# The mixers' sample products on whole zero-padded operands, level products regrouped, diagonal scores from a ones product

## The chip, the core and the metric

The kernel runs on one NeuronCore of a Trainium2 chip. That core has five engines with a queue each: TensorE (PE; its weight loads are shown as PEld), VectorE (DVE), ScalarE (ACT), GpSimd (POOL) and SyncE (SP), which here only issues DMAs. The metric is the device time of one execution in microseconds (us), lower is better.

## The reference, cut to what matters

One inference step of a two-layer encoder. Two sequences go through the same weights: a prompt of 256 frames and a sample of 32 frames, which continues a stream with a recurrent state and cached keys and values. Each layer is a half SwiGLU, a mixer, and another half SwiGLU, each on normalised input and added to x. Layer 0 has the mixer AB: 8 HGRN2 heads and 8 stick-breaking attention heads side by side. Layer 1 has the mixer C, a gMLP with a spatial product over positions.

```
# HGRN2, blocks of positions; c = cumulative sum of log f, k = 1 - f
scores = einsum('bthc,btshc,bshc->bhts', q, decay, k)       # s <= t
o      = scores @ v + (q * exp(c)) @ S
S_new  = exp(c_last) * S + (k * exp(c_last - c))^T @ v
# stick-breaking: A[t,s] = sigmoid(z_ts) * prod_{s<j<t} (1 - sigmoid(z_tj)), o = A @ v
# gMLP: mixed = ws @ layernorm(v) + b ; out = (u * mixed) @ w_out
```

All is float32 to the outside. The outputs are y of both sequences, the new keys and values, the new HGRN states and the sample's normalised v rows.

## The kernel before, in words

Activations lie with features on the 128 partitions and the NT = 288 tokens in the columns: columns 0 to 31 are the sample, 32 to 287 the prompt's two blocks of 128. Weights are streamed from DRAM in chunks of up to 8 x 128 rows and 256 columns; ScalarE and VectorE split every chunk into a rounded part `wh` and a rest `wl` (lines 169 and 170), and for each 128x128 block TensorE makes three products with 288 columns (lines 209 to 211: `wl` with the rounded activations, `wh` with their rest, `wh` with the rounded ones) into `acc`. These are 9216 products, and they are called weight products below.

The mixers' own work runs beside them in lanes: generators (`hgrn`, `stick_keys`, `stick`, `spatial`) of which a step is taken every so many row blocks of a chunk (`tick`, line 187). A step issues a few small products, which so stand as a short block between two weight products in TensorE's queue, and the work of the other engines around them. The order of every queue is fixed when the program is built (a scheduler may move instructions that don't depend on each other); at run time each engine takes its queue in order and waits on semaphores.

In mixer AB there are four head pairs p. For each, `hgrn` makes:

- the diagonal of the scores (lines 537 to 540): per head b, a product of k and q for each of the prompt's two blocks and one of 32x32 for the sample, of which only the diagonal is kept (lines 543, 544). The second prompt block has its sources back to front, for which `kr` holds k mirrored;
- seven levels m = 1 to 64 (`scores`, line 511): per head one product of 128x128x128 for the prompt and, in the five levels up to m = 16, one with a stationary of 32 columns for the sample (line 518), in turn head by head; `place` puts them into `sc` and `ss` by a mask;
- the states (line 579) from decayed keys `kt` and values `vt`, the outputs (lines 594 to 598), and their transposes back (line 617). The sample's share of these takes 32 rows (or columns) of a tile only: `ROWS = (P, P, TS)`.

`stick_keys` transposes the normalised keys (line 672, again 128, 128 and 32 rows), `stick` sums the sample's queries' squares (line 706, after head 1's transposes and squares) and `weighted` makes the outputs, where the sample's new values are a stationary of 32 rows (line 776). In mixer C, `spatial` multiplies the normalised v with the spatial weights: two products of 128x128x128 for the prompt (line 895) and one with 32 rows for the sample (line 896), in 16 blocks.

A product of two float32 operands that are not rounded is recorded as two matmuls, a transpose and a weight product as one. The matmul's shape in a row is written rows*columns of the stationary operand in the array.

Of the kernel before, what the change touches and what calls it, by code (L numbers as in the profile page):

```python
# [10 lines left out]
AF = mybir.ActivationFunctionType  # L11
# [15 lines left out]
LEVELS = (1, 2, 4, 8, 16, 32, 64)   # HGRN: block lengths; up to 16 a mask picks the blocks  # L27
NM = 5

# token windows of 128 columns: the prompt's blocks, and one that the sample leads  # L30
WIN = ((32, 160), (160, 288), (0, 128))
ROWS = (P, P, TS)


def shape_constants():
    """Masks and identity: they depend on shapes alone."""
    ident = np.eye(P, dtype=np.float32)
    s = np.arange(P)[:, None]
    t = np.arange(P)[None, :]
    ge = (s <= t).astype(np.float32)          # [query, key]: key >= query  # L40
# [6 lines left out]
    # level masks [source, target of a second half]; the second block's sources are back to front  # L47
# [11 lines left out]
class Lane:  # L59
    """Work that runs beside the weight products, a step at a time."""  # L60
# [19 lines left out]
class Net:  # L80
# [66 lines left out]
    def fetch_half(self, j):  # L147
        """The first chunk, half of its rows at a time."""
# [6 lines left out]
    def pieces(self, i):  # L155
        """The steps that split chunk i, a few row blocks each."""
# [30 lines left out]
    def tick(self):  # L187
        """Between row blocks: the next chunk's split and the lanes' steps go on."""
# [7 lines left out]
    def mm(self, acc, ch, rhs, order, first, last, blocks=(0, 1)):  # L196
        """acc[:, b] (+)= the chunk's column block b times rhs; order: (row block, rhs block)."""
# [36 lines left out]
    def put(self, k, h):  # L234
        """Two hidden blocks from k on, split into two parts."""
# [6 lines left out]
    def gained(self, k, x, g):  # L242
        """Block k of the next products' operand, gain * x, in two parts."""
# [5 lines left out]
    def square(self, k):  # L249
        """The squares' sum over the blocks of x; after the last, 1 / rms."""  # L250
# [11 lines left out]
    def rnorm(self, sq):  # L262
        """1 / rms of each token, on every partition: rb [128, 2, NT]."""
# [26 lines left out]
    def resid(self, j, b, acc, scale, gnext):  # L290
        """Block 2j + b of x takes the product up."""
# [17 lines left out]
    def out_proj(self, plan, scale, gnext, j0=0):  # L309
        """x += scale * (hidden @ w): plan: the K chunks' orders."""  # L310
# [41 lines left out]
    # column groups of ab_w_in, as they are taken: f, q, v, gate of HGRN; v, k, q of stick-breaking  # L352
# [14 lines left out]
    def mixer_ab(self, gnext):  # L367
        nc, I = self.nc, self.I
        with self.tc.tile_pool(name="ab", bufs=1, reuse_waits="tile") as pool:
# [10 lines left out]
            nc.gpsimd.memset(self.sk, 1.0)  # L380
            self.gk = T("gk", [P, P])
# [56 lines left out]
    def hgrn(self, p, pool, d):  # L438
        """Two heads. The prompt in two chunks of 128 positions, the sample in one of 32. In a chunk,
        decays between positions are products of f within blocks of m positions, m doubling:  # L440
        Pp[t] = f from t's block start through t, E[s] = f from after s to its block's end."""
# [24 lines left out]
        vt = T("vt", [P, 2, 384])  # L466
# [673 lines left out]
```

## Time and profile before

| what | value |
|---|---|
| time of one execution, 3 runs | 1382.73, 1382.88, 1384.78 us (median 1382.88) |
| span of the profiled execution, first to last instruction | 1381.3 us |
| TensorE, matmuls | 1374.0 us busy, 99% of the span, 10234 records |
| VectorE | 872.5 us, 63% |
| ScalarE | 658.8 us, 48% |
| GpSimd | 83.6 us, 6% |
| granted TensorE clock, mean | 1.000 |
| HBM traffic | 154 GB/s over the span |

The page has no execution time of the profiled run beside its span; the median of the timed runs is 1.6 us above the span. Busy time of an engine counts the union of its records. Matmuls overlap in the pipeline and their ends are modelled, so how long a product holds the queue is read from the starts of neighbouring records, not from a record's length.

### The profile page before, as it was taken

The page shows a single profiled execution, that of the slowest core. Times are in us where ns is not written, and L with a number is a line of the kernel's source. Part 1 is how long each engine was busy: PE and PEld are TensorE (multiplying, and loading weights), DVE is VectorE, ACT ScalarE, POOL GpSimd, SP SyncE. Part 2 cuts the span into 40 slices and gives each one's busy share as a digit, 9 for nine tenths or more (in the row PEclk, how much of TensorE's full clock was granted, in tenths as well). Part 3 has the DMA queues.
Part 4 walks back from the last instruction along what each step waited for, and adds up shares of the span by engine and source line. Part 5 has one row for each costly group of instructions (what it writes and reads, how often), then busy time and mean ns, then how long its engine had stood idle before and what let it go on. Part 6 is the DMA issues. An engine that isn't in the chain of part 4 may idle for free.

```text
span 1381.3 us, 24967 instructions
## 1 busy us (share of the span) xinstructions
PE 1374.0 (99%) x10234; PEld 1341.9 (97%) x10234; DVE 872.5 (63%) x1623; ACT 658.8 (48%) x1343; POOL 83.6 (6%) x133
## 2 busy tenths in 40 slices
PE   9999999999999999999999999999999999999998
PEld 8999999989898989999999999999999999999998
DVE  7666557767676756666665666655568865666643
ACT  6444445373736455544444444444554445444432
POOL 0000000010101010000000100000110910000000
PEclk9999999999999999999999999999999999999999
DMA  8454555343434334654545745454544445555451
GB/s 286 156 182 154 164 163 186 119 158 100 144 114 130 94 115 134 196 168 154 182 139 167 218 153 183 153 162 160 175 139 137 149 141 157 172 160 174 155 178 48
DMA packets 212788, 214.71 MB, mean 155 GB/s; under 512 B 4737, under 2 KB 211314, under 8 KB 212674
## 3 DMA queue, kind: packets, MB, share of 16 engines
q1 hardware_dynamic: 211314, 210.56, 47.7%
q0 software_dynamic: 672, 1.90, 0.5%
q8 instruction: 80, 1.31, 0.4%
q10 hardware_dynamic: 688, 0.66, 0.2%
q14 instruction: 34, 0.28, 0.1%
HBM read 208.25 MB, written 4.85 MB: 154 GB/s over the span
## 4 chain that ended last, share of the span: by engine, by line
PE 97%; ACT 1%; DMA 1%; DVE 1%; SPq 0%; issue 0%; POOL 0%; ACTq 0%
PE acc L209 30%; PE acc L211 29%; PE acc L210 29%; PE sc L515 1%; DMA wraw<-in_ffn_w_up_dram 1%; PE vt L126 1%; PE sp L895 1%; PE S L579 0%; PE sc L518 0%; ACT on L702 0%; PE sp L896 0%; PE kt L126 0%; ACT on L600 0%; PE zs L720 0%; PE oT L617 0%; PE kn L672 0%
## 5 line engine op out<-in xcount | busy, mean ns | idle before, releaser
L169 ACT CAST wh<-wraw 128x512 fp32r<-128x512 f32 x768 | 442.2, 619 | 540.8 <-PE acc L211 412.4
L170 DVE TENSOR_TENSOR wl<-wraw,wh 128x512 fp32r<-128x512 f32 x768 | 507.8, 688 | 270.1 <-ACT wh L169 269.8
L209 PE MATMUL acc<-xh,wl 128*128 128x288 f32 x2112 | 638.6, 302 | 0.0
L211 PE MATMUL acc<-xh,wh 128*128 128x288 f32 x2112 | 623.9, 295 | 0.0
L210 PE MATMUL acc<-xl,wh 128*128 128x288 f32 x2112 | 621.9, 294 | 0.0
L209 PEld LDWEIGHTS acc<-xh,wl 128*128 128x128 f32 x2112 | 397.4, 188 | 4.4 <-issue 1.4
L210 PEld LDWEIGHTS acc<-xl,wh 128*128 128x128 f32 x2112 | 398.4, 189 | 1.2 <-issue 0.5
L211 PEld LDWEIGHTS acc<-xh,wh 128*128 128x128 f32 x2112 | 397.3, 188 | 0.0
L209 PE MATMUL acc<-hh,wl 128*128 128x288 f32 x960 | 285.5, 298 | 0.0
L210 PE MATMUL acc<-hl,wh 128*128 128x288 f32 x960 | 283.1, 295 | 0.0
L211 PE MATMUL acc<-hh,wh 128*128 128x288 f32 x960 | 283.0, 295 | 0.0
L209 PEld LDWEIGHTS acc<-hh,wl 128*128 128x128 f32 x960 | 180.3, 188 | 1.1 <-issue 0.2
L210 PEld LDWEIGHTS acc<-hl,wh 128*128 128x128 f32 x960 | 180.5, 188 | 0.1
L211 PEld LDWEIGHTS acc<-hh,wh 128*128 128x128 f32 x960 | 180.3, 188 | 0.0
L227 DVE TENSOR_TENSOR u<-acc,rb 128x576 f32<-128x576 f32 x52 | 39.3, 756 | 52.1 <-PE acc L211 52.0
L227 DVE TENSOR_TENSOR g<-acc,rb 128x576 f32<-128x576 f32 x48 | 36.3, 757 | 49.1 <-PE acc L211 48.7
L238 ACT CAST hh<-u 128x576 fp32r<-128x576 f32 x52 | 35.1, 674 | 54.1 <-DVE u L347 39.3
L239 DVE TENSOR_TENSOR hl<-u,hh 128x576 fp32r<-128x576 f32 x52 | 39.6, 762 | 7.8 <-ACT hh L238 1.8
L119 POOL TENSOR_TENSOR pw<-ms,mhalf 128x3 f32<-128x3 f32 x6 | 6.4, 1069 | 534.5 <-DVE ms L272 515.9
L245 ACT ACTIVATE xh<-xT,cols 128x288 fp32r<-128x288 f32 x40 | 21.3, 532 | 26.7 <-DVE xT L298 15.4
L347 DVE TENSOR_TENSOR u<-u,g 128x576 f32<-128x576 f32 x44 | 33.1, 752 | 0.0
L345 ACT ACTIVATE g<-g 128x576 f32<-128x576 f32 x44 | 29.9, 679 | 2.5 <-DVE g L227 2.5
(244 smaller groups left out, 831.4 us busy)
## 6 DMA issues: line engine op xcount, KB each, us to landing
wraw<-in_ffn_w_up_dram SPq DMA_DIRECT2D x44, 1024.0 KB, 5.7
wraw<-in_ffn_w_gate_dram SPq DMA_DIRECT2D x43, 1024.0 KB, 5.5
wraw<-in_ffn_w_down_dram SPq DMA_DIRECT2D x32, 1024.0 KB, 5.4
wraw<-in_ab_w_in_dram SPq DMA_DIRECT2D x28, 1024.0 KB, 5.1
wraw<-in_c_w_in_dram SPq DMA_DIRECT2D x16, 1024.0 KB, 5.4
wraw<-in_ffn_w_down_dram SPq DMA_DIRECT2D x16, 768.0 KB, 4.6
wraw<-in_c_w_out_dram SPq DMA_DIRECT2D x8, 1024.0 KB, 5.1
wraw<-in_ab_w_out_dram SPq DMA_DIRECT2D x8, 768.0 KB
```

The source lines that it names most:

```text
L126: self.nc.tensor.transpose(pv[:, i * P:i * P + P], x[:, b, s:e], self.ident)
L169: self.nc.scalar.copy(out=h[:, x], in_=w[:, a:b])
L170: self.nc.vector.tensor_tensor(out=l[:, x], in0=w[:, a:b], in1=h[:, x].bitcast(F32), op=ALU.subtract)
L209: mm(o, lhsT=l[:, k, c], rhs=hi[:, r], start=st, stop=False)
L210: mm(o, lhsT=h[:, k, c], rhs=lo[:, r], start=False, stop=False)
L211: mm(o, lhsT=h[:, k, c], rhs=hi[:, r], start=False, stop=en)
L227: self.nc.vector.tensor_tensor(out=x, in0=acc[:, :, :NT], in1=self.rb, op=ALU.mult)
L238: nc.scalar.copy(out=hh, in_=h)
L239: nc.vector.tensor_tensor(out=self.hl[:, k:k + 2], in0=h, in1=hh.bitcast(F32), op=ALU.subtract)
L245: nc.scalar.activation(out=self.xh[:, k], in_=x, func=AF.Copy, scale=g)
L345: nc.scalar.activation(out=g, in_=g, func=AF.Silu)
L347: nc.vector.tensor_tensor(out=u, in0=u, in1=g, op=ALU.mult)
```

## The change

It does four things.

1. The sample's operands become whole 128x128 tiles, whose unused part is zero or not read: new tiles `vz` (values), `ss` (scores) and `ws` (stick-breaking weights), set to zero once on GpSimd at the start of mixer AB, and `wsS` in mixer C. ScalarE writes the sample's values into `vz` by a copy of its own. The state, output and spatial products and the transposes then take 128 rows and columns; a new helper `to_cols` transposes the sample's window first and lets the first prompt block overwrite what it wrote beyond its 32 columns.
2. In `scores` the two heads' wide products come first and then the two narrow ones, which stay 32 columns wide.
3. The diagonal: GpSimd multiplies q and k elementwise (`qk`, 128x576), and one product per head with a stationary of ones (288 columns) replaces the three products.
4. The sample's query squares (before: line 706) are summed right after the transposes of head 0.

The removal of comments, which is the rest of the diff, is left out here.

```diff
+    def to_cols(self, to, rows):
+        for w in (2, 0, 1):
+            s, e = WIN[w]
+            self.nc.tensor.transpose(to[:, s:e], rows(w), self.ident)
...
+            self.vz, self.ss, self.ws = T("vz", [P, 2, P]), T("ss", [P, 2, P]), T("ws", [P, 3, 64])
+            for x in (self.vz, self.ss, self.ws):
+                nc.gpsimd.memset(x, 0.0)
...
+        qk = T("tmp")
+        nc.gpsimd.tensor_tensor(out=qk, in0=q, in1=k, op=mul)
...
-            nc.scalar.copy(out=vt[:, b], in_=pv[:, :384])
+            nc.scalar.copy(out=vt[:, b], in_=pv[:, :TP])
+            nc.scalar.copy(out=vz[:TS, b], in_=pv[:TS, TP:384])
...
                 mm(ps[:, b * P:b * P + P], lhsT=QK[:, b, 32:160], rhs=QK[:, b, 160:], start=True, stop=True)
-                if m <= 16:
+            if m <= 16:
+                for b in range(2):
                     x = QK[:, b, 0:TS]
...
-            mm(ps[:, 0:128], lhsT=k[:, b, 32:160], rhs=q[:, b, 32:160], start=True, stop=True)
-            mm(ps[:, 128:256], lhsT=kr[:, b], rhs=q[:, b, 160:], start=True, stop=True)
-            mm(ps[:TS, 256:288], lhsT=k[:, b, 0:TS], rhs=q[:, b, 0:TS], start=True, stop=True)
+            mm(ps[:, :NT], lhsT=self.ones, rhs=qk[:, b], start=True, stop=True)
...
-            for w, n in enumerate(ROWS):
+            for w, x in enumerate((vt[:, b, 0:P], vt[:, b, P:], vz[:, b])):
                 c = slice(w * P, w * P + P)
-                mm(pn[:, c], lhsT=kt[:n, c], rhs=vt[:n, b, c], start=True, stop=True)
+                mm(pn[:, c], lhsT=kt[:, c], rhs=x, start=True, stop=True)
...
-            mm(o[:TS, 256:384], lhsT=ss[:, b], rhs=vt[:TS, b, 256:384], start=True, stop=False)
-            mm(o[:TS, 256:384], lhsT=q[:, b, 0:TS], rhs=S0[:, b], start=False, stop=True)
+            mm(o[:, 256:384], lhsT=ss[:, b], rhs=vz[:, b], start=True, stop=False)
+            mm(o[:, 256:384], lhsT=q[:, b, 0:P], rhs=S0[:, b], start=False, stop=True)
...
-                nc.scalar.activation(out=on[:n, w * P:w * P + P], in_=po[b][:n, w * P:w * P + P], func=AF.Copy,
-                                     scale=rs[:n, 3 * b + w:3 * b + w + 1])
+                nc.scalar.activation(out=on[:, w * P:w * P + P], in_=po[b][:, w * P:w * P + P], func=AF.Copy,
+                                     scale=rs[:, 3 * b + w:3 * b + w + 1])
...
-                nc.tensor.transpose(pt[:, WIN[w][0]:WIN[w][0] + n], on[:n, w * P:w * P + P], self.ident[:n, :n])
+            self.to_cols(pt, lambda w: on[:, w * P:w * P + P])
...
-                nc.tensor.transpose(pn[:, s:s + n], kt[:n, w, b], self.ident[:n, :n])
+            self.to_cols(pn, lambda w: kt[:, w, b])
...
+            if b == 0:
+                for i in range(2):
+                    mm(pt[TS * i:TS * i + TS, TP:TP + 1], lhsT=sq[:, i], rhs=self.ones[:, 0:1], start=True, stop=True)
+                nc.vector.tensor_copy(out=ms[:64, 12:13], in_=pt[:64, TP:TP + 1])
...
-        mm(po[:, 0:TS], lhsT=vt[:TS, 2, b], rhs=ws[:TS, 2, tc], start=False, stop=True)
+        mm(po[:, 0:TS], lhsT=vt[:, 2, b], rhs=ws[:, 2, tc], start=False, stop=True)
...
-                    mm(p[:, 0:TS], lhsT=vt[:TS, 2, c:c + P], rhs=wsS[:, n], start=True, stop=True)
+                    mm(p[:, 0:TS], lhsT=vt[:, 2, c:c + P], rhs=wsS[:, n], start=True, stop=True)
```

Three places show how the queues move. The first is TensorE's queue in head pair 0 at the diagonal and the first level, before; `sc` is the tile of scores, QK the decayed keys and queries, the acc rows are weight products, and the sizes are those of the output.

```order
L211 MATMUL acc_2719<-xh,wh_2692 128x288
L538 MATMUL sc_2809<-q_2651,k_2743 128x128
L539 MATMUL sc_2809<-q_2651,kr_2762 128x128
L540 MATMUL sc_2809<-q_2651,k_2743 32x32
...
L515 MATMUL sc_2878<-QK_2813 128x128
L518 MATMUL sc_2878<-QK_2813 32x16
L515 MATMUL sc_2878<-QK_2813 128x128
L518 MATMUL sc_2878<-QK_2813 32x16
```

The same place in the changed program; `tmp` holds GpSimd's product of q and k.

```order
L218 MATMUL acc_2725<-xh,wh_2698 128x288
L556 MATMUL sc_2818<-tmp_2770,ones 128x288
L216 MATMUL acc_2829<-xh,wl_2735 128x288
...
L529 MATMUL sc_2883<-QK_2820 128x128 x2
L533 MATMUL sc_2883<-QK_2820 32x16 x2
```

Three products have become one, and the level's wide and narrow products stand together, two and two, so the narrow shape is entered once and not twice.

The second place is TensorE's queue in head pair 0 where head 0's outputs `on` are transposed into `oT`; `zs` are the sample's attention scores, `ss` the squares' sums. Before:

```order
L209 MATMUL acc_3266<-xh,wl_3209 128x288
L706 MATMUL ss_3340<-ones,sq_3317 32x1 x2
L210 MATMUL acc_3266<-xl,wh_3208 128x288
L211 MATMUL acc_3266<-xh,wh_3208 128x288
L209 MATMUL acc_3408<-xh,wl_3276 128x288
L617 MATMUL oT_3392<-ident,on_3382 128x128
L720 MATMUL zs_3397<-pkT_3051,bq_3140 32x256
L617 MATMUL oT_3392<-ident,on_3382 128x128
L617 MATMUL oT_3392<-ident,on_3382 128x32
L721 MATMUL zs_3397<-kn_3050,bq_3140 32x32
```

The changed program:

```order
L216 MATMUL acc_3413<-xh,wl_3281 128x288
L217 MATMUL acc_3413<-xl,wh_3280 128x288
L218 MATMUL acc_3413<-xh,wh_3280 128x288
L216 MATMUL acc_3413<-xh,wl_3281 128x288
L217 MATMUL acc_3413<-xl,wh_3280 128x288
L134 MATMUL oT_3397<-ident,on_3387 128x128 x3
L733 MATMUL zs_3402<-pkT_3056,bq_3145 32x256
L734 MATMUL zs_3402<-kn_3055,bq_3145 32x32
```

The squares' block is gone from here, the three transposes stand together, four weight products later in the chunk than before, and the first of them is now the sample's window, which ScalarE writes last.

The third place is GpSimd's queue from head pair 0 to 1; E are decays, pw reciprocal roots, Bz attention weights to be masked. Before:

```order
L464 MEMSET E_3567 128x576
L119 TENSOR_TENSOR pw_3133<-ks_3131,mhalf 128x6
L119 TENSOR_TENSOR pw_3360<-oms_3358,mhalf 128x6
L119 TENSOR_TENSOR pw_3370<-sk_2484,mhalf 128x5
L739 AFFINE_SELECT Bz_3434<-Bz_3434 128x2x128
```

The changed program:

```order
L477 MEMSET E_3573 128x576
L119 TENSOR_TENSOR pw_3138<-ks_3136,mhalf 128x6
L119 TENSOR_TENSOR pw_3365<-oms_3363,mhalf 128x6
L119 TENSOR_TENSOR pw_3375<-sk_2484,mhalf 128x5
L475 TENSOR_TENSOR tmp_3571<-q_3411,k_3538 128x576
L752 AFFINE_SELECT Bz_3439<-Bz_3439 128x2x128
```

The product of q and k for the next head pair stands ahead of the select that masks this pair's attention weights.

## Rows read from the trace of the kernel before

**Rows 1.** The chain that ended last, shares of the span by engine.

```profile
PE 97%; ACT 1%; DMA 1%; DVE 1%; SPq 0%; issue 0%; POOL 0%; ACTq 0%
```

**Rows 2.** TensorE's waits: who waited for whom, total us, times, longest.

```profile
PE ss L706 <- ACT on L702: 0.8, 4, 0.2
```

**Rows 3.** Stretches: us, busy us (records) of PE PEld DVE ACT POOL, clock, DMA, GB/s.

```profile
318.00:389.00 71.00, 70.81 (x521) 64.99 (x520) 50.32 (x123) 38.12 (x109) 5.51 (x6) 1.00 0.39 124
...
565.00:776.00 211.00, 211.00 (x1592) 210.86 (x1591) 126.78 (x205) 97.15 (x172) 0.85 (x1) 1.00 0.52 165
...
1078.00:1092.00 14.00, 14.00 (x103) 13.35 (x102) 13.18 (x22) 5.96 (x11) 13.26 (x24) 1.00 0.45 150
```

**Rows 4.** Timeline of TensorE, a level with narrow products: start us, length us, instruction.

```profile
263.67 0.39 PE L515 MATMUL sc<-QK 128*128 128x128 f32 x2
263.99 0.23 PE L518 MATMUL sc<-QK 128*32 128x16 f32 x2
264.15 0.49 PE L515 MATMUL sc<-QK 128*128 128x128 f32 x2
264.57 0.24 PE L518 MATMUL sc<-QK 128*32 128x16 f32 x2
...
264.97 0.30 PE L210 MATMUL acc<-xl,wh 128*128 128x288 f32 x1
```

**Rows 5.** Timeline of TensorE, a level of wide products alone.

```profile
277.83 0.61 PE L515 MATMUL sc<-QK 128*128 128x128 f32 x4
...
278.41 0.29 PE L210 MATMUL acc<-xl,wh 128*128 128x288 f32 x1
```

**Rows 6.** Timeline of TensorE, a ones product of 288 columns, and the diagonal.

```profile
230.69 0.65 PE L283 MATMUL rb<-dg,ones 128*128 128x288 f32 x2
...
231.31 0.29 PE L210 MATMUL acc<-xl,wh 128*128 128x288 f32 x1
...
322.33 0.38 PE L538 MATMUL sc<-q,k 128*128 128x128 f32 x2
...
323.28 0.29 PE L210 MATMUL acc<-xl,wh 128*128 128x288 f32 x1
```

**Rows 7.** Timeline of TensorE, states, then key transposes (128, 128, 32 rows).

```profile
288.80 1.02 PE L579 MATMUL S<-vt,kt 128*128 128x128 f32 x6
...
289.99 0.30 PE L210 MATMUL acc<-xl,wh 128*128 128x288 f32 x1
...
290.65 0.56 PE L672 MATMUL kn<-ident,bkt 128*128 128x128 f32 x3
...
291.37 0.30 PE L210 MATMUL acc<-xl,wh 128*128 128x288 f32 x1
```

**Rows 8.** Timeline of TensorE, outputs of one head.

```profile
292.04 0.38 PE L594 MATMUL o<-vt,sc 128*128 128x128 f32 x2
...
293.70 0.29 PE L210 MATMUL acc<-xl,wh 128*128 128x288 f32 x1
```

**Rows 9.** Timeline of TensorE, a spatial block of mixer C.

```profile
1068.23 0.61 PE L895 MATMUL sp<-wsT,vt 128*128 128x128 f32 x4
...
1069.34 0.30 PE L210 MATMUL acc<-xl,wh 128*128 128x288 f32 x1
```

**Rows 10.** Timeline of TensorE, end of a block of stick-breaking outputs.

```profile
527.40 0.53 PE L775 MATMUL ob<-ws,pv 128*128 128x32 f32 x4
...
528.43 0.29 PE L211 MATMUL acc<-hh,wh 128*128 128x288 f32 x1
```

**Rows 11.** Timeline, ScalarE's scaling of head 0's outputs and their first transpose.

```profile
300.40 0.86 ACT L612 ACTIVATE on<-o,pw 128x128 f32<-128x128 f32 x3
...
301.02 0.27 PE L617 MATMUL oT<-ident,on 128*128 128x128 f32 x1
```

**Rows 12.** Timeline of VectorE, head pair 1's q.

```profile
305.46 0.75 DVE L460 TENSOR_TENSOR q<-q,tmp 128x576 f32<-128x576 f32 x1
```

**Rows 13.** Groups by shape on GpSimd: count | busy us, mean ns | idle before.

```profile
L905 POOL TENSOR_TENSOR z<-z,BS 128x160 f32<-128x160 f32 x16 | 10.0, 628 | 1.0
```

More of the change, by code (lines that the diff above doesn't have):

```diff
@@ L523, in place @@
             if m <= 16:
-                for to, lv, fr in ((sc, self.lv, ps[:, 0:256]), (ss, self.ls, ps[:TS, 256:288])):
-                    nc.vector.copy_predicated(
-                        to.rearrange("p h (n two m) -> p (h n) two m", two=2, m=m)[:, :, 1],
-                        lv[:, i].rearrange("p (n m) -> p n m", m=m), fr.rearrange("p (n m) -> p n m", m=m))
+                nc.vector.copy_predicated(
+                    sc.rearrange("p h (n two m) -> p (h n) two m", two=2, m=m)[:, :, 1],
+                    self.lv[:, i].rearrange("p (n m) -> p n m", m=m), ps[:, 0:256].rearrange("p (n m) -> p n m", m=m))
+                by_head = lambda a: a.rearrange("p (h n m) -> p h n m", h=2, m=m)
+                nc.vector.copy_predicated(
+                    ss[:TS, :, :TS].rearrange("p h (n two m) -> p h n two m", two=2, m=m)[:, :, :, 1],
+                    by_head(self.ls[:, i]), by_head(ps[:TS, 256:288]))
                 return
@@ L610, in hgrn @@
             on = T("on", [P, 384])
-            for w, n in enumerate(ROWS):
-                nc.scalar.activation(out=on[:n, w * P:w * P + P], in_=po[b][:n, w * P:w * P + P], func=AF.Copy,
-                                     scale=rs[:n, 3 * b + w:3 * b + w + 1])
+            for w in range(3):
+                nc.scalar.activation(out=on[:, w * P:w * P + P], in_=po[b][:, w * P:w * P + P], func=AF.Copy,
+                                     scale=rs[:, 3 * b + w:3 * b + w + 1])
             yield
             pt = self.ps("oT")
-            for w, n in enumerate(ROWS):
-                nc.tensor.transpose(pt[:, WIN[w][0]:WIN[w][0] + n], on[:n, w * P:w * P + P], self.ident[:n, :n])
+            self.to_cols(pt, lambda w: on[:, w * P:w * P + P])
             go = self.gc["go"] + h
@@ L659, in stick_keys @@
         for b in range(2):
-            for w, n in enumerate(ROWS):
-                nc.vector.scalar_tensor_tensor(out=kt[:n, w, b], in0=pts[b][:n, w * P:w * P + P],
-                                               scalar=r[:n, 2 * w + b:2 * w + b + 1], in1=self.gk[:n], op0=mul, op1=mul)
+            for w in range(3):
+                nc.vector.scalar_tensor_tensor(out=kt[:, w, b], in0=pts[b][:, w * P:w * P + P],
+                                               scalar=r[:, 2 * w + b:2 * w + b + 1], in1=self.gk, op0=mul, op1=mul)
             pt = self.ps("pkT")
@@ L669, in stick_keys @@
             pn = self.ps("kn")
-            for w, n in enumerate(ROWS):
-                s = WIN[w][0]
-                nc.tensor.transpose(pn[:, s:s + n], kt[:n, w, b], self.ident[:n, :n])
+            self.to_cols(pn, lambda w: kt[:, w, b])
             nc.scalar.copy(out=kn[:, b], in_=pn[:, :NT])
@@ L703, in stick @@
                                      accum_out=ms[:, i:i + 1])
-            if b == 1:
-                for i in range(2):
-                    mm(pt[TS * i:TS * i + TS, TP:TP + 1], lhsT=sq[:, i], rhs=self.ones[:, 0:1], start=True, stop=True)
-                nc.vector.tensor_copy(out=ms[:64, 12:13], in_=pt[:64, TP:TP + 1])
             yield
@@ L748, in stick @@
             yield
-        ws = T("ws", [P, 3, 64])
+        ws = self.ws
         pw = self.ps("wTs")
@@ L823, in spatial_weights @@
                     yield
-                nc.scalar.copy(out=wsS, in_=wsT[:TS, :, :TS])
+                nc.scalar.copy(out=wsS[:TS], in_=wsT[:TS, :, :TS])
                 nc.vector.memset(wsT[64:, :, 0:64], 0.0)
@@ L832, in spatial_weights @@
                 pt = self.ps("RS")
-                mm(pt[:, :8 * TS], lhsT=self.ones[:TS], rhs=wsS, start=True, stop=True)
+                mm(pt[:, :8 * TS], lhsT=self.ones, rhs=wsS, start=True, stop=True)
                 nc.scalar.copy(out=rs[:, :, P:], in_=pt[:, :8 * TS].rearrange("p (g i) -> p g i", i=TS))
```

11 lines of the change are left out of this document (6 added, 5 removed).

## The prediction

> **What bounds the kernel now.** I read the chain that ended last first: TensorE holds 97% of the span [rows 1]. Then its waits: the largest that comes back is 0.2 us, four times, where the query squares wait for ScalarE [rows 2]. Then a stretch of SwiGLU without mixer work: 1592 matmuls in 211.00 us, TensorE busy throughout at a granted clock of 1.00 [rows 3]. So the kernel is TensorE's queue laid end to end, at 211.00 / 1592 = 0.1325 us a weight product, and its time changes by what the mixers' blocks hold of that queue. The last view is the timeline of TensorE at these blocks: the reader is to see not the lengths of records, which overlap, but the distance from a block's start to the start of the second weight product after it (the first still runs late behind the block), less 0.13 us for the one weight product in between. I call that a block's price.
>
> **Prices in the trace.** Four wide records of two level products: 278.41 - 277.83 - 0.13 = 0.45 us, 0.11 us a record [rows 5]. The level with narrow products, also 128x128 stationaries for the prompt but with 32-column ones between them: 264.97 - 263.67 - 0.13 = 1.17 us for eight records [rows 4]. Within it, the first wide pair holds 0.32 us (two records of 0.11 and 0.10 more), the narrow pair 0.16 us, the second wide pair 0.42 us (0.20 more), the last narrow pair 264.97 - 264.57 - 0.13 = 0.27 us. So it is not the narrow records' work that costs, but going from the 128x128 shape to another and back: about 0.1 us each way.
>
> The Trainium skill has a sentence for this, in "TensorEngine Tiling (Array Packing)", Key Properties: "Changing tiling mode (not just tile) drains the TensorE". This case's trace agrees, with the 0.10 us beside each change of shape.
>
> **The change part by part.** A block that becomes all wide is priced at 0.11 us a record.
>
> - Levels, 5 in each of 4 head pairs, 20 blocks. The wide four with one way out hold 0.45 + 0.10 = 0.55 us; the last narrow pair with the way back 0.27 us, as now; the first narrow pair without a way back is not in the trace: between 0 and the 0.16 us which it holds with one. I take 0.10, nearer to the row. Together 0.92 us, 0.25 less. 20 x 0.25 = 5.0 us (3.8 to 7.0 by the ends).
> - Diagonal, 8 blocks. Now 323.28 - 322.33 - 0.13 = 0.82 us; a product of 288 columns with a stationary of ones holds 231.31 - 230.69 - 0.13 = 0.49 us [rows 6]. 8 x 0.33 = 2.6 us.
> - States, 8 blocks of six records. Now 289.99 - 288.80 - 0.13 = 1.06 us [rows 7], then 6 x 0.11 = 0.67. 8 x 0.39 = 3.1 us.
> - Outputs, 8 blocks of ten records. Now 293.70 - 292.04 - 0.13 = 1.53 us [rows 8], then 1.11. In four of them q's transposes follow and share the way back, so I take 0.40 and not 0.42. 8 x 0.40 = 3.2 us.
> - Transposes of keys and of outputs, 16 blocks of three records. Now 291.37 - 290.65 - 0.13 = 0.59 us [rows 7], then 0.33: 16 x 0.26 = 4.2; four stand behind a states block whose way back is counted above, so 4.0 us.
> - Spatial products, 16 blocks of six records. Now 1069.34 - 1068.23 - 0.13 = 0.98 us [rows 9], then 0.67. 16 x 0.31 = 5.0 us.
> - Stick-breaking outputs, 8 blocks, of which the last six records change (two of 32 rows become 128): now 528.43 - 527.40 - 0.13 = 0.90 us [rows 10], then 0.67. 8 x 0.23 = 1.8 us. The records before have two products of 32 moving columns only and are wide already, and in the price of 0.67 they count like the others.
> - Query squares: moved ahead of the squares on ScalarE for which they wait, 4 x 0.2 = 0.8 us [rows 2]. They stay narrow and keep their ways in and out.
>
> The sum is 25.5 us.
>
> **What is late next.** The output transposes of head 0. Before, TensorE starts the first at 301.02, and ScalarE finishes the third piece of `on` at 300.40 + 0.86 = 301.26 [rows 11]; the late pieces were transposed behind other products. In the changed queue the three stand together, the sample's piece, ScalarE's last, first. TensorE comes there at 301.02, plus four weight products (0.53), less the squares' block with its wait (0.6) and the 0.40 of the outputs block before it: about 300.55. ScalarE's piece hangs by squares and a power on the same outputs block, of which ten records' gain comes 0.3 us earlier: 300.96. That is a new wait of 0.4 us in each of the 4 pairs, 1.6 us (0 if the chain in between shortens as much, 2.5 at most by these rows).
>
> **What is added elsewhere.** GpSimd's product of q and k, 128x576: not in the trace. GpSimd's two-operand product of 128x160 takes 0.63 us in the mean [rows 13]; between that and 576/160 of it, 2.3 us, I take 2.3. q of the next pair is ready at 305.46 + 0.75 = 306.21 [rows 12] and its diagonal comes at 322.33 [rows 6]: 16 us of cover. Queued behind it on GpSimd is the select of the current pair's attention weights, for which VectorE's product waits, and behind that VectorE's splits of weights; VectorE is busy 50.32 of 71 us in such a pair [rows 3], so 2 us are caught up there before TensorE asks. Without that cover it would be 3 pairs x 2 us. ScalarE's 8 copies of `vz` (38.12 of 71 us busy) and the four memsets, at mixer starts on a GpSimd with 5.51 of 71 us of work, lie beside TensorE's work: nothing. SyncE's queue has nothing new.
>
> Net: 25.5 - 1.6 = 23.9 us. The profiled execution's span is 1381.3; the runs' median is 1.6 above it. 1381.3 - 23.9 = 1357.4, and with the 1.6 us 1359.0 us.
>
> **The rivals.**
>
> First, mixer C gives its 5.0 us back. Between 1078 and 1092 GpSimd is busy 13.26 and VectorE 13.18 of 14 us [rows 3], both on `spatial`; if they set its pace, TensorE's shorter blocks end in waits for PSUM tiles that VectorE has not read. 1359.0 + 5.0 = 1364.0. For it: these two numbers. Against: TensorE waits for neither of them there now, and the stretch is short, with lighter ones after it.
>
> Second, padding doesn't help where the moving operand is short: a shape of 32 columns still costs, whatever the stationary. Then the spatial products and stick-breaking outputs keep their price: 1359.0 + 5.0 + 1.8 = 1365.8 us. Against: four records of 128*128 with 32 columns stand in the block of [rows 10] and the six with them come to 0.90, just 0.23 over six plain ones.
>
> Third, slower than before: narrow records are the cheap ones, and the 0.1 us belong to the end of any block, not to the shape. Then 112 narrow records (16 states, 32 outputs, 16 transposes, 32 spatial, 16 stick-breaking) become wide and each pays 0.11 instead of half of the 0.16 us of a narrow pair with its way back, so about 0.06 more at the least [rows 4, 5], up to 0.11: 112 x 0.06 = 6.7 us. The levels gain nothing, the diagonal and the squares' wait give 3.4 back, the new wait takes 1.6: 1382.9 + 6.7 - 3.4 + 1.6 = 1387.8 us. It decides from a padded record of 0.32 us on, which would eat all 23.9 us. Against: the ten records of an outputs block at 0.11 would be 1.11, its four narrow ones make it 1.53, so they cost more than wide ones, about 0.2 each [rows 8].
>
> The Trainium skill's page "TensorEngine Tiling (Array Packing)", Theoretical Speedup, speaks for this third way: a dimension of at most 32 allows a tiling factor of four, so small operands should be tiled, not padded. By that rule a padded record would cost up to four narrow ones; the trace disagrees here, since the products of this kernel come singly and no other tile works beside them.
>
> **How the numbers follow.** My forecast has 0.80, the first rival 0.08, the second 0.07, the third 0.03; 0.02 is left for a queue that stalls somewhere I don't see, with a time about as before. The forecast's own ends: levels 2.0 better and no new wait 1.6 give 1355.4; levels 1.2 worse, the wait 0.9 worse and 1 us of small waits in blocks that now come earlier give 1362.1. The range takes in the first rival: 1355 to 1364.5. 0.2% of the time is 2.8 us, about what a measurement of this kernel can tell from no change; all but the last two cases are far beyond it, so faster 0.95, same 0.02, slower 0.03.
>
> **What would show it.** In the changed profile the shapes 32*32 and 32*128 are gone from lines of states, outputs, keys, spatial and stick-breaking outputs; a level holds 0.92 us instead of 1.17; a states block 0.67, an outputs block 1.11, a spatial block 0.67; and TensorE's waits list the output transposes on ScalarE with about 0.4 us four times, and no squares. VectorE and GpSimd should be as busy in us as before, but for some 9 us more on GpSimd. I am wrong if a block of all-wide records still has 0.1 us at its end, if the ones product waits for GpSimd, or if weight products in the mixers wait for `wl`.

## The result, and the profile after

The changed kernel takes 1356.98 us (median of 4 runs, 1356.74 to 1359.61), the kernel before beside it 1383.08 us. The ratio is 0.9813, with a 95% interval of 0.9801 to 0.9826. The prediction was 1359.0 us with a range of 1355 to 1364.5. The span of the profiled execution went from 1381.3 to 1355.0 us, 26.3 less; the sum had 23.9.

Line numbers below are those of the changed kernel: the weight products are lines 216 to 218. First the shares of the chain that ended last, then TensorE's largest wait in total (total us, times, longest), the counterparts of [rows 1, 2].

```profile
PE 96%; ACT 1%; DMA 1%; DVE 1%; POOL 0%; issue 0%; SPq 0%; POOLq 0%; ACTq 0%
```

```profile
PE oT L134 <- ACT on L628: 1.4, 4, 0.4
```

TensorE is still the bound. The squares' wait is gone, and the wait foreseen at the output transposes stands there, four times 0.4 us at most. The other waits are at the kernel's start and end, as before. TensorE waits for nothing in mixer C. Two stretches, with the columns of [rows 3]; the second lies as far behind mixer C's first spatial product as the one shown there:

```profile
565.00:776.00 211.00, 211.00 (x1592) 210.86 (x1592) 127.11 (x206) 95.71 (x172) 4.23 (x5) 1.00 0.55 170
1056.40:1070.40 14.00, 14.00 (x112) 14.00 (x112) 13.15 (x23) 5.43 (x10) 13.26 (x24) 1.00 0.47 152
```

The SwiGLU stretch holds the same 1592 matmuls, at the same clock of 1.00. In mixer C 112 matmuls now fit into 14 us, where 103 did, with VectorE and GpSimd as full as before (13.15 and 13.26 us). Over the whole execution VectorE is busy 874.2 us instead of 872.5, and GpSimd 95.0 instead of 83.6: 11.4 us more, where the prediction had some 9. The product takes 8.8 of them, the new memsets 1.2, and the selects of the attention weights went from 4.4 to 6.0.

Now the blocks, read as in the prediction: the start of the second weight product behind the block, less the block's start, less 0.13 us. First TensorE's timeline at a level with narrow products, the counterpart of [rows 4].

```profile
256.10 0.61 PE L529 MATMUL sc<-QK 128*128 128x128 f32 x4
256.64 0.30 PE L533 MATMUL sc<-QK 128*32 128x16 f32 x4
...
257.11 0.29 PE L217 MATMUL acc<-xl,wh 128*128 128x288 f32 x1
```

A level holds 257.11 - 256.10 - 0.13 = 0.88 us (0.87 in the mean of the 20) where 0.92 was predicted. The ones product, and states, key transposes and outputs [rows 6 to 8]:

```profile
251.16 0.65 PE L556 MATMUL sc<-tmp,ones 128*128 128x288 f32 x2
...
251.78 0.29 PE L217 MATMUL acc<-xl,wh 128*128 128x288 f32 x1
...
286.24 0.61 PE L595 MATMUL S<-vt,kt 128*128 128x128 f32 x4
...
287.04 0.29 PE L217 MATMUL acc<-xl,wh 128*128 128x288 f32 x1
...
287.70 0.49 PE L134 MATMUL kn<-ident,bkt 128*128 128x128 f32 x3
...
288.17 0.30 PE L217 MATMUL acc<-xl,wh 128*128 128x288 f32 x1
...
288.83 0.38 PE L610 MATMUL o<-vt,sc 128*128 128x128 f32 x2
...
290.08 0.29 PE L217 MATMUL acc<-xl,wh 128*128 128x288 f32 x1
```

These come to 0.49, 0.67, 0.34 and 1.12 us; the prediction had 0.49, 0.67, 0.33 and 1.11. A spatial block and the end of a stick-breaking block [rows 9, 10]:

```profile
1044.14 0.61 PE L909 MATMUL sp<-wsT,vt 128*128 128x128 f32 x4
1044.58 0.31 PE L910 MATMUL sp<-wsS,vt 128*128 128x32 f32 x2
...
1044.94 0.30 PE L217 MATMUL acc<-xl,wh 128*128 128x288 f32 x1
```

```profile
506.61 0.53 PE L788 MATMUL ob<-ws,pv 128*128 128x32 f32 x4
506.97 0.39 PE L789 MATMUL ob<-ws,bvt 128*128 128x32 f32 x2
...
507.41 0.29 PE L218 MATMUL acc<-hh,wh 128*128 128x288 f32 x1
```

Both hold 0.67 us, as predicted, and there the shape is 128*128 although the moving operand has 32 columns.

The one block that surprised is that of the output transposes with the sample's attention scores `zs`. Before, as a continuation of [rows 11]:

```profile
301.23 0.62 PE L720 MATMUL zs<-pkT,bq 128*32 128x256 f32 x2
301.78 0.50 PE L617 MATMUL oT<-ident,on 128*128 128x128 f32 x2
302.21 0.22 PE L721 MATMUL zs<-kn,bq 128*32 128x32 f32 x1
...
303.06 0.30 PE L211 MATMUL acc<-xh,wh 128*128 128x288 f32 x1
```

After, with the weight product ahead of the block; in brackets the idle time before the record and what ended it:

```profile
297.16 0.29 PE L217 MATMUL acc<-xl,wh 128*128 128x288 f32 x1
297.80 0.55 PE L134 MATMUL oT<-ident,on 128*128 128x128 f32 x3 [0.34 <-ACT on L628]
298.27 0.63 PE L733 MATMUL zs<-pkT,bq 128*32 128x256 f32 x4
298.73 0.24 PE L734 MATMUL zs<-kn,bq 128*32 128x32 f32 x4
...
299.13 0.29 PE L216 MATMUL acc<-xh,wl 128*128 128x288 f32 x1
```

The block held 303.06 - 301.02 - 0.13 = 1.91 us before and holds 299.13 - 297.80 - 0.13 = 1.20 now, 0.71 less, of which the sum had 0.26 for the transposes. The other 0.45, 1.8 us in four pairs, was not foreseen: the narrow `zs` products are entered once, and the two heads' products, whose results go to PSUM partitions 0 to 31 and 32 to 63, stand next to each other. Single records of the two heads start 13 ns apart there.

The price leaves out the wait ahead of the block. By starts it costs the queue more than its 0.34 us of idle time: 297.80 - 297.16 - 0.13 = 0.51 us, about 2.0 us in the four pairs.

Last, what the product on GpSimd did to VectorE: a group on GpSimd (count | busy us, mean ns | idle before), then the timelines in head pair 1: GpSimd's product, VectorE, and TensorE's next use of VectorE's `v`.

```profile
L475 POOL TENSOR_TENSOR tmp<-q,k 128x576 f32<-128x576 f32 x4 | 8.8, 2197 | 25.5 <-DVE q L471 20.9 <-PE acc L218 4.6
```

```profile
302.80 2.36 POOL L475 TENSOR_TENSOR tmp<-q,k 128x576 f32<-128x576 f32 x1 [4.58 <-PE acc L218]
```

```profile
303.84 1.60 DVE L507 TENSOR_TENSOR QK<-q,f 128x256 f32<-128x256 f32 x1
...
310.08 0.81 DVE L403 TENSOR_TENSOR v<-acc,rb 128x320 f32<-128x320 f32 x2
```

```profile
311.13 0.49 PE L126 MATMUL vt<-ident,v 128*128 128x128 f32 x3
```

The product takes 2.2 us in the mean (estimate: 2.3). VectorE's operation beside it takes 1.60 us; its like took 0.40 before. The rows of before, with `v` and its transposes:

```profile
307.84 0.40 DVE L493 TENSOR_TENSOR QK<-q,f 128x256 f32<-128x256 f32 x1
...
312.13 0.81 DVE L392 TENSOR_TENSOR v<-acc,rb 128x320 f32<-128x320 f32 x2
```

```profile
315.86 0.49 PE L126 MATMUL vt<-ident,v 128*128 128x128 f32 x3
```

And v, which VectorE writes in two halves for TensorE, is done at 310.08 + 0.81 = 310.89 and transposed from 311.13 on. Before, it was done at 312.13 + 0.81 = 312.94 and transposed at 315.86. A margin of 2.9 us has become 0.2, without a wait yet. GpSimd's product is only a part of this: TensorE, its own queue being shorter, arrives 4.7 us earlier, and v only 2.05 us earlier.

### The profile page after: what moved, and what is told of

It is laid out like the page before. It is cut to its first block, busy times and chain, and to the rows that moved or that the text cites. A ratio compares the mean times of both kernels' runs of the same rounds, so it can differ in the third digit from the quotient of the medians.

```text
span 1355.0 us, 24939 instructions
## 1 busy us (share of the span) xinstructions
PE 1346.8 (99%) x10202; PEld 1332.1 (98%) x10202; DVE 874.2 (65%) x1623; ACT 657.8 (49%) x1351; POOL 95.0 (7%) x141
## 4 chain that ended last, share of the span: by engine, by line
PE 96%; ACT 1%; DMA 1%; DVE 1%; POOL 0%; issue 0%; SPq 0%; POOLq 0%; ACTq 0%
PE acc L216 30%; PE acc L218 30%; PE acc L217 29%; PE sc L529 1%; DMA wraw<-in_ffn_w_up_dram 1%; PE vt L126 1%; PE sp L909 1%; PE S L595 0%; POOL pw L119 0%; PE kt L126 0%; ACT wh L176 0%; PE sc L533 0%; PE sc L556 0%; PE oT L134 0%; PE z L745 0%; PE ob L784 0%
## 5 line engine op out<-in xcount | busy, mean ns | idle before, releaser
L252 ACT ACTIVATE xh<-xT,cols 128x288 fp32r<-128x288 f32 x40 | 21.3, 531 | 25.5 <-DVE xT L305 15.4
```

What stands on the lines that cost most here:

```text
L252: nc.scalar.activation(out=self.xh[:, k], in_=x, func=AF.Copy, scale=g)
```

## The experiments

My theory: TensorE's queue is the time, a block's price is its records at 0.11 us and 0.1 us for every change of shape, and the rest of the change is hidden. The rivals are those of the prediction, and for the added GpSimd work, that its cover is thinner than I argued. Medians of 4 to 9 runs, ratios with a 95% interval to the kernel before in the same session. Its median there was 1384.45 us beside e1 to e4, and 1382.9 to 1383.1 beside the others, so a gain is read from the ratio or from spans and not from two medians of different sessions.

**e1: the regrouped levels alone.** The kernel before with one edit:

```diff
-                if m <= 16:
+            if m <= 16:
+                for b in range(2):
```

> The kernel before, with only the two heads' level products regrouped: wide, wide, narrow, narrow in place of wide, narrow, wide, narrow. The same records, nothing padded, nothing left out. Theory (going from the 128x128 shape to another and back costs about 0.1 us each way, the narrow record itself little): the 20 blocks go from 1.17 to about 0.87 us, so 6 us less, 1377 us, and the block's fifth to eighth record follow each other within 0.06 us. Rival (a narrow product costs by itself, wherever it stands; the gain of the changed kernel came from padding and from fewer records): no change, 1383 us.

Measured: 1377.25 us, ratio 0.9950 (0.9938 to 0.9963); span 1375.1, 6.2 less than before, with the waits of before. A level holds 0.87 us here too: 20 x 0.30 = 6.0. The theory holds.

**e2: the diagonal alone.** The kernel before with GpSimd's product and the ones product, as in the diff of the change (`qk = T("tmp")` to `rhs=qk[:, b]`).

> The kernel before, with only the diagonal taken from GpSimd's product and a ones product. Theory: 8 blocks from 0.82 to 0.49 us, 2.6 us less, 1380.5 us; GpSimd's product of about 2.2 us stays hidden. Rival (GpSimd's product holds up VectorE, and the splits or the attention weights come late): a wait on TensorE in three head pairs that eats the gain, 1383 us or more.

Measured: 1380.44 us, ratio 0.9976 (0.9967 to 0.9986); span 1378.7, 2.6 less, no new wait. As expected.

**e3: mixer C's padding alone.** The kernel before with `wsS` made 128 rows high, zero outside the sample and read whole by its row sums, and with

```diff
-                    mm(p[:, 0:TS], lhsT=vt[:TS, 2, c:c + P], rhs=wsS[:, n], start=True, stop=True)
+                    mm(p[:, 0:TS], lhsT=vt[:, 2, c:c + P], rhs=wsS[:, n], start=True, stop=True)
```

> The kernel before, with only mixer C's sample operands made whole 128x128 tiles. Theory: 16 spatial blocks from 0.98 to 0.67 us and one block of row sums 0.3 us shorter, 5.3 us less, 1377.8 us. Rivals: GpSimd and VectorE set the pace of that stage, or a short moving operand of 32 columns costs whatever the stationary is: both no change, 1383 us; the first with waits of TensorE in the stage, the second with spatial blocks still at 0.98 us.

Measured: 1379.48 us, ratio 0.9960 (0.9946 to 0.9973); span 1379.0. By the ratio that is 3.7 to 7.5 us less than the kernel before beside it, around the 5.3 expected. The span is only 2.3 us below that of before, but not for a rival's reason. Its spatial blocks:

```profile
1069.87 0.60 PE L896 MATMUL sp<-wsT,vt 128*128 128x128 f32 x4
...
1070.67 0.29 PE L210 MATMUL acc<-xl,wh 128*128 128x288 f32 x1
```

1070.67 - 1069.87 - 0.13 = 0.67 us each, 16 x 0.31 = 5.0 us less, and TensorE waits for nothing in the stage. But at the start it waits for an input, and the stretch behind that wait has the columns of [rows 3]:

```profile
PE x L998 <- DMA xs<-in_x_prompt_dram: 1.5, 1, 1.5
```

```profile
6.00:14.00 8.00, 7.56 (x31) 5.86 (x32) 6.02 (x12) 3.82 (x8) 0.00 (x0) 0.59 1.09 353
```

Behind the wait the granted clock was 0.59 and TensorE made 31 records; in the same 8 us of the kernel before it made 46 at a clock of 1.00. The first transposes of v then stand at 250.17 instead of 247.87, 2.3 us later. The kernel's start differs in this way by 1 or 2 us from build to build and from run to run, and here it hides part of the gain. The first rival (VectorE and GpSimd pace mixer C) and the second (short moving operands cost anyway) fall by the blocks, not by the time.

**e4: GpSimd's product four times.** The changed kernel with

```diff
-        nc.gpsimd.tensor_tensor(out=qk, in0=q, in1=k, op=mul)
+        for _ in range(4):
+            nc.gpsimd.tensor_tensor(out=qk, in0=q, in1=k, op=mul)
```

> The changed kernel, with GpSimd's product of q and k made four times over into the same tile (three times for nothing). If the cover is the 16 us from q to the diagonal, as the prediction had it first, 6.6 us more of it are still hidden: 1357 us. If the cover is that of the select queued behind it on GpSimd, whose masked weights TensorE transposes about 2.0 us after VectorE has them, then 3 more products of 2.2 to 2.4 us make TensorE wait about 4.9 us at these transposes in each of 3 head pairs: about 1371 us.

Measured: 1376.63 us, span 1374.6, 19.6 more than the changed kernel. More than either theory had. A wait, then TensorE's timeline behind it, then two stretches of head pair 1 (columns of [rows 3]):

```profile
PE vt L126 <- DVE v L403: 10.4, 4, 3.0
```

```profile
317.56 1.02 PE L126 MATMUL vt<-ident,v 128*128 128x128 f32 x3 [3.00 <-DVE v L403]
```

```profile
313.00:317.00 4.00, 1.56 (x12) 1.32 (x10) 4.00 (x6) 1.62 (x3) 2.62 (x2) 1.00 0.00 0
317.00:321.00 4.00, 3.44 (x15) 3.11 (x15) 3.97 (x11) 0.93 (x3) 0.00 (x0) 0.57 0.17 45
```

What was late is v, not what I had named. And 10.4 us of waits cost 19.6, mostly because after each of the three waits of 3 us the granted clock fell: in head pair 1 it was 1.00 before the wait and 0.57 over the 4 us behind it, so at 1.2 GHz for most of them, and in the other two pairs 0.66 and 0.58. The three transposes take 1.02 us instead of 0.49. The wait in head pair 0 was shorter, and over the 4 us behind it the clock stayed at 1.00:

```profile
251.11 0.33 PE L126 MATMUL vt<-ident,v 128*128 128x128 f32 x1 [1.39 <-DVE v L403]
```

(The expectation of e11 calls this wait 1.7 us, which is the distance of the two starts; the idle time is 1.4.)

**e5: the padding of mixer AB alone.** The changed kernel with regrouping, diagonal and mixer C's padding undone, by the reverse of the lines shown for e1 to e3.

> The changed kernel with the regrouping, the diagonal and mixer C put back as before: what is left is the padding in mixer AB and the earlier squares. By the prediction's terms: states 3.1, outputs 3.2, transposes 4.0, stick-breaking outputs 1.8, squares 0.8, less the new wait of 1.4 to 1.6: about 11.5 us less than before. With the three others alone (block prices 5.9, 2.6 and 5.3 us) the parts then add up to the whole of 26 us. Rival (the parts share a gain, or one hides another's wait): the sum of the four misses the whole by 3 us or more.

Measured: 1370.47 us, ratio 0.9912 (0.9898 to 0.9926); span 1368.8, 12.5 less, with the new wait of 1.4 us in it. That is 1 us more than expected, as the unforeseen gain of the `zs` products lies in this part. The four parts give 6.2 + 2.6 + 5.3 (e3 by its blocks, with the sums of its spatial weights) + 12.5 = 26.6, against 26.3 for the whole: they add up to within 0.3 us, so no part's gain hangs on another by more than that.

**e6: the narrow level products once.** The changed kernel; the sample's decayed operands of the levels are kept in one tile, and their products made in one block behind the last of them.

```diff
-            if m <= 16:
-                for b in range(2):
-                    x = QK[:, b, 0:TS]
+            if m == 16:
+                px.append(self.ps("scs"))
+                for i in range(NM):
+                    for b in range(2):
+                        x = QS[:, i, b] if i < NM - 1 else QK[:, b, 0:TS]
...
+                        mm(px[0][:TS, c:c + 16], lhsT=x,
```

> The changed kernel, with the sample's level products of a head pair kept for one block after level 16: the same 80 narrow records, but one way into and out of the narrow shape in a head pair in place of five. Theory: four of five levels at 0.45 us, the fifth at 0.54 and 20 narrow records at about 0.04 each with the way back 1.0 us, 3.3 in place of 4.35 us: 4 x 1.0 = 4 us less than the changed kernel, 1353 us. Rival (narrow records cost 0.08 each by their own, and the ways little): under 1 us, 1356 us or more.

Measured: 1352.09 us, ratio 0.9779 (0.9765 to 0.9792). The narrow records of the block:

```profile
267.64 0.68 PE L542 MATMUL scs<-QS 128*32 128x16 f32 x16
268.17 0.28 PE L542 MATMUL scs<-QK 128*32 128x16 f32 x4
```

Sixteen narrow records take 268.17 - 267.64 = 0.53 us, 33 ns each, a third of a wide one. Entering and leaving the shape was the cost, as the theory says, and not the narrow records: a fifth of the entries gives 4.9 us (4.0 expected).

**e7: the sample's outputs scaled first.** The changed kernel, to take away the wait of 1.4 us, with ScalarE's three pieces in the order in which TensorE transposes them.

```diff
-            for w in range(3):
+            for w in (2, 0, 1):
```

> The changed kernel, with ScalarE scaling the sample's piece of the outputs first, in the order in which TensorE transposes the pieces. If the new wait of 0.35 us, four times, is for ScalarE's third piece, the first transpose is ready two pieces (about 0.6 us) earlier, the third then two transposes (0.2 us) after it: the wait falls to about 0.15, or is gone, and up to 1 us in all is won, 1356 us. Rival (the wait is for the power on GpSimd ahead of all three pieces): the wait falls by no more than what the pieces' order gives, and some 0.1 to 0.2 us stay.

Measured: 1360.78 us, 3.8 more than the changed kernel; ratio 0.9838 (0.9824 to 0.9851). A miss, and a telling one:

```profile
299.22 0.33 PE L134 MATMUL oT<-ident,on 128*128 128x128 f32 x1 [0.36 <-ACT on L628]
299.48 0.62 PE L733 MATMUL zs<-pkT,bq 128*32 128x256 f32 x2
300.03 0.44 PE L134 MATMUL oT<-ident,on 128*128 128x128 f32 x2
...
301.25 0.30 PE L218 MATMUL acc<-xh,wh 128*128 128x288 f32 x1
```

With the first piece earlier, the scheduler lets TensorE take it earlier, so it waits as long, and puts the narrow `zs` products between the transposes again, as before the change. The block is back at 301.25 - 299.22 - 0.13 = 1.90 us: 4 x 0.70 = 2.8 us. The other 1 us is in the kernel's start: in the profiled execution (span 1359.7) v's first transposes stand 1.9 us later than in the changed kernel. This is also the test of the unforeseen 1.8 us, and it says more than that. Here the transposes are padded and the `zs` products stand apart, and the block holds 1.90 us; before, with narrow transposes and the `zs` products apart too, it held 1.91. So in these four blocks padding alone gave next to nothing, and standing together gives the whole 2.8 us.

**e8: e6 and e7 together**, and the sample's squares from one stationary of 128 columns.

> The changed kernel with both edits above (narrow level products once in a head pair, the sample's piece first) and the squares of the sample's queries from a whole 128x128 stationary. Theory: 4 us, about 0.8 us and 4 x 0.13 = 0.5 us: 1351.7 us. Rival: VectorE's added products for the sample (about 0.2 us in each of 20 levels) or the five masked copies in a row bring waits of TensorE at the level products that take 2 us or more of this back.

Measured: 1354.21 us, ratio 0.9796 (0.9783 to 0.9809). 2.1 us above e6. Its `zs` block holds 1.90 us again, so it carries e7's loss of 2.8 us, less 0.5 for the squares (e9).

**e9: e6 with the squares, without e7.**

```diff
-                for i in range(2):
-                    mm(pt[TS * i:TS * i + TS, TP:TP + 1], lhsT=sq[:, i], rhs=self.ones[:, 0:1], start=True, stop=True)
+                mm(pt[:, TP:TP + 1], lhsT=sq, rhs=self.ones[:, 0:1], start=True, stop=True)
```

> The changed kernel with the narrow level products once per head pair (as in the run before that did only this) and with the squares of the sample's queries summed from one whole 128x128 stationary tile, zero outside the 64 columns in use, in the place of two stationaries of 32 columns. ScalarE's order of the output pieces is left alone. My theory, in which a change of shape costs about 0.1 us each way: the two small squares products leave a block of transposes that is otherwise all wide, 4 times, so about 0.15 us less each, 0.6 us in all: 1352.1 - 0.6 = about 1351.5 us, and the sample's scores of stick-breaking still stand right behind the output transposes. The rival, that the order of TensorE's queue decides more than the shapes: with any edit of this block the scheduler sets the scores apart again and 3 us or more come on top, 1354 to 1355 us.

Measured: 1351.72 us, ratio 0.9772 (0.9759 to 0.9786). The `zs` products stayed behind the transposes. The gain of 0.4 us on e6 is within what the runs scatter; in the trace the block with the squares shrinks from 0.57 to 0.44 us, 0.5 us in four pairs, as the theory had it.

**e10: e9 with head 1's narrow products on other partitions.**

```diff
-                        mm(px[0][:TS, c:c + 16], lhsT=x,
+                        mm(px[0][TS * b:TS * b + TS, 16 * i:16 * i + 16], lhsT=x,
```

> As the run beside it, and in the block of narrow level products head 1's results go to PSUM partitions 32 to 63 in place of 0 to 31, so that the two heads' products stand in different column groups of the array; the masked copies become two per level. My theory: neighbours in different column groups start some 13 ns apart, as the two heads' stick-breaking score products did in the changed kernel, instead of 32 to 52 ns; 12 products of two records then hold about half, 0.3 to 0.4 us less per head pair: 4 x 0.35 = 1.4 us less than the run beside it, about 1350.1 us, and the block of 24 records shrinks from 1.27 to about 0.9 us. The rival: products alternate between column groups record by record (two records each), or a narrow record costs the same wherever its result goes, or VectorE's five extra small copies come late for the outputs: then the block stays at 1.27 us and the time within 0.5 us of the run beside it, or above it.

Measured: 1350.25 us, ratio 0.9758 (0.9745 to 0.9772), the best of all. The narrow records of the block:

```profile
268.35 0.43 PE L542 MATMUL scs<-QS 128*32 128x16 f32 x16
268.63 0.22 PE L542 MATMUL scs<-QK 128*32 128x16 f32 x4
```

Sixteen records now take 268.63 - 268.35 = 0.28 us, 17 ns each instead of 33: with the other four 20 x 16 ns = 0.3 us less in each block, 1.3 in all, of the 1.5 measured. The Trainium skill's page "TensorEngine Tiling (Array Packing)", Key Properties, says that different tiles of the array can work in parallel. Here the trace agrees: results on other partitions, with TensorE's products otherwise as in e9, halve the records' distance. So the idea that the prediction weighed against its own pays once several small products stand together, by a factor of two with two groups (four were not tried); for the single products of this kernel padding was the faster.

**e11: GpSimd's product twice.** As e4, with `range(2)`.

> The changed kernel with GpSimd's product of q and k made twice in place of once. My theory after the run with four: what the product costs is VectorE's time beside it (there three more products, 4.97 us, stretched VectorE's next operations by 3.7 us, 0.74 us a us), and the first thing that is late is v, which in the changed kernel VectorE finishes only 0.2 us before TensorE transposes it in head pairs 1 to 3, and 1.8 us before in pair 0. One product more, 1.7 to 2.2 us, stretches VectorE by 1.2 to 1.6 us: waits of 1.0 to 1.4 us for v in three pairs and none in pair 0, 3.0 to 4.2 us, and no fall of the granted clock, as the wait of 1.7 us in the run with four brought none. About 1360.6 us (1360.0 to 1361.2). The rival, my prediction's own reason: the product has 16 us of cover until its diagonal is needed, and the 2 us are caught up before TensorE asks, so only the pile of three products hurt: 1357 us, no wait for v.

Measured: 1359.51 us, 2.5 more than the changed kernel; ratio 0.9831 (0.9818 to 0.9845).

```profile
PE vt L126 <- DVE v L403: 1.8, 3, 0.6
```

```profile
311.62 0.77 PE L126 MATMUL vt<-ident,v 128*128 128x128 f32 x3 [0.60 <-DVE v L403]
```

The wait for v is there in three pairs, so the rival (16 us of cover) falls. The time is below the range that I gave, as I had the wait too long, at 1.0 to 1.4 us: v comes 1.0 us later than in the changed kernel, and the transposes begin when its first half is written, so the margin was 0.4 to 0.5 us and not 0.2. The three transposes behind a wait take 0.77 instead of 0.49 us, since the second of them needs v's second half: 0.8 us in all, which with the 1.8 makes 2.6.

**e12: the product on VectorE.** The changed kernel with

```diff
-        nc.gpsimd.tensor_tensor(out=qk, in0=q, in1=k, op=mul)
+        nc.vector.tensor_tensor(out=qk, in0=q, in1=k, op=mul)
```

> The changed kernel with the product of q and k on VectorE in place of GpSimd (TensorE's queue is the same, row for row). VectorE gets 0.75 us more per pair, and its operations beside GpSimd's product are no longer stretched (1.60 instead of 0.42 us for one, 0.74 instead of 0.55 for another). In this kernel the order of VectorE's queue moves too: v is evacuated ahead of the next level's decayed queries. My theory, in which TensorE's queue alone sets the time as long as nothing is late: 1357.0 us, within 0.5 us, no wait for v, and v done over 1 us before TensorE asks in place of 0.2. The rival: VectorE's queue is tight at this place, and what moved behind v (decayed queries of the first level) is late for TensorE instead: waits of a level's products for VectorE in 3 or 4 pairs, 1358 to 1361 us.

Measured: 1356.51 us, ratio 0.9812 (0.9798 to 0.9825), the same as the changed kernel. VectorE's and TensorE's rows at v:

```profile
311.29 0.82 DVE L403 TENSOR_TENSOR v<-acc,rb 128x320 f32<-128x320 f32 x2
```

```profile
313.87 0.49 PE L126 MATMUL vt<-ident,v 128*128 128x128 f32 x3
```

v is done 1.8 us before TensorE takes it, and nothing else is late in mixer AB. (These rows are of an execution of 1359.42 us, the longest of the four, which lost time in the kernel's start.) VectorE needs 0.73 us for the product that takes GpSimd 2.2, and is rid of the 1.2 us by which that stretched it: the engine is no busier (872.1 us instead of 874.2). Of the 2.7 us of margin that the change took, 1.6 come back without GpSimd's product. The other 1.1 lie in TensorE's shorter queue and VectorE's own 0.73 us; no run separates these two.

## Why the prediction was right, and where it was not

- What bounds the kernel, and the prices in the trace: right. In six kinds of block the all-wide records came to 0.11 us each, within 0.01 us. With every record counted from its start to the next one's, what stands between weight products shrank from 131.2 to 104.5 us, and the weight products, waits behind them included, stayed (1244.9 and 1245.3).
- Levels: the mechanism right, the size small. The first narrow pair, which the trace didn't show without a way back, holds 0.05 us and not 0.10; about 6 us instead of 5.0 (e1: 6.2).
- Diagonal 2.6, states 3.1, outputs 3.2, spatial 5.0, stick-breaking 1.8: as predicted (after's rows, e2, e3). The sum left out 0.3 us for the row sums of mixer C's sample weights, which are padded too.
- Transposes, 4.0 us: 12 of the 16 blocks gave their 3.0 us by padding, as predicted. The four with the `zs` products gave 2.8 us, of which the sum had 1.0, and by e7 not for the reason in the sum. The order showed the `zs` products standing together behind the transposes, and the prediction read from it the wait but not what adjacency saves. That the sum had something for these blocks at all was luck.
- The new wait: foreseen at 1.6 us. It came as 1.4 us of idle time, and by starts it costs the queue 2.0. It is not cured by ScalarE's order (e7). Likewise the squares' wait of 0.8 us cost the queue 1.4 before, and their narrow pair in its new place holds 0.09 us more, four times.
- With these sizes the sum is 25.5 + 1.0 + 0.3 + 1.8 for levels, row sums and `zs`, + 0.6 - 0.4 for the squares, - 2.0 for the wait: 26.8 us, against 26.3 in the span. The 0.5 us between them stay open; they are less than the scatter of the kernel's start. The forecast's 23.9 was 2.4 us short: the levels and the `zs` products make 2.8 of that, and the other terms nearly cancel.
- GpSimd's product: costs nothing, as said, but by luck, since the step "16 us of cover" named the wrong reader. Not the diagonal is late first, but v, behind VectorE operations that the product holds up: 2.9 us of margin became 0.2 (0.4 to 0.5 for the first half), partly by the product and partly by TensorE's shorter queue (e11, e12). One product more made v 1.0 us later and cost 2.5 us (e11).
- The rivals: C's pace and short moving operands fall by e3's blocks; "narrow records are cheap" is half right. They are, at 33 ns in a row (e6), but going to them is not, so padding wins for single products. For twenty of them in a row the prices speak for the narrow shape: the block of e6 holds 1.38 us, of which 0.93 are the narrow records with their ways, and twenty padded records at 0.11 would hold 2.2; padding them was not run.

## What to carry to other kernels

On a queue without waits, count how often the shape of the stationary operand changes, not how small the products are: pad a lone small product to the neighbours' shape, and collect small products that can wait into one block, with neighbours on different output partitions. Read from the order which narrow products stand together, since a harmless edit elsewhere can part them again. For work added to GpSimd, ask what VectorE does beside it and which of its results TensorE needs next; the added result's own reader may be the last to be late.

## What the hardware showed that I had not expected

A VectorE product of two operands beside GpSimd's product took 1.60 instead of 0.40 us; e4's product on GpSimd stretched a scan of 128x384 from 0.94 to 2.18. The Trainium skill's page "SBUF — State Buffer", Summary: rules for kernel authors, says that when a VectorE instruction has two inputs in SBUF while GpSimd's reads SBUF, the second to issue is blocked until the first has finished. For the product the trace agrees: the 1.60 us run from 303.84 to 305.44, and GpSimd's product from 302.80 to 305.16, so most of the 0.40 us of work came when it ended. A scan that VectorE began at 302.98, 0.18 us after GpSimd's record, still took only 0.94 us, and GpSimd's record is longer (2.36 us) than those of its repeats in e4 (1.43 to 1.76), as if GpSimd had waited for the scan; no run separates the two.

Three waits of 3 us on TensorE cost far more than their length, since the granted clock over the 4 us behind them was 0.57 to 0.66 (e4). Behind a wait of 1.4 us it stayed at 1.00 (e4), and waits of 0.6 us brought no fall of the clock over the execution, 1.00 (e11).
